# A block of four mixers and a gated FFN on one core: one difference of the fast down projection made later, five of its chunks moved ahead of the last pair's values, and another order in the input norm

## Chip, cores and metric

One Trainium2 chip, one of its cores. The metric is the time of one execution on the device in microseconds (us), as the median of the runs of a kernel; all numbers of the trace come from one profiled execution. The engines have short names in the profile: PE is TensorE (matmuls), PEld its weight loads, DVE is VectorE, ACT is ScalarE, POOL is GpSimd, SP is SyncE, which here only issues DMAs. A "q" behind a name is the engine's sequencer.

## What is computed

One layer over 1024 tokens of width 1024, in float32. Four mixers, the gates, two norms and the FFN; what matters here is the input norm and the FFN.

```python
h = rms_norm(x, norm_mix_g)
proj = h @ w_in                    # all branches and the gates
...                                # four mixers, gated and merged
x = x + merged @ w_out
h = rms_norm(x, norm_ffn_g)

def conv_ffn(h, w_up, conv_w, conv_b, w_down):
    up = causal_dwconv(h @ w_up, conv_w) + conv_b
    val, gate = jnp.split(up, 2, axis=-1)
    return (jax.nn.silu(gate) * val) @ w_down

x = x + conv_ffn(h, ffn_w_up, ffn_conv_w, ffn_conv_b, ffn_w_down)   # D_FF = 2816
return rms_norm(x, norm_final_g)
```

## The kernel before

**Number format.** Every float32 operand of a large matmul is split into a rounded high part and the rest (`split`, L153: a cast, then a subtraction of 128x512), and a product is three matmuls: high by high, low by high, high by low. Tiles named `...hi` and `...lo`, `th` and `tl` are such parts. Channels lie on the partitions, tokens along the free axis.

**Order of the work.** The program is traced in Python order, and a scheduler then lays out each engine's queue at compile time: an instruction that stands earlier in the program has the higher priority, and a later one may be put ahead of it where the scheduler expects the earlier one to have to wait. On the chip every engine runs its own queue in order. A tile's buffer is reused when its last reader is done; pools that are opened after others have closed take their memory.

**Input norm** (`norm_in`, L349). x comes in two halves of 512 tokens. For each half x times the gain is split unscaled, the products of block B_DN and of the first two gate blocks are made from it, and only then the row scale is known (`rms_scale`, a sum of squares by PE and a chain of twelve small VectorE instructions); `spread_scale` brings it to the rows by eight small matmuls, and the products are scaled behind (`scaled`). `rescale` (L406) multiplies x by gain and scale and splits it again for all later products: the cast on ScalarE, the low part on VectorE for k = 0, 3, 6 and on GpSimd for the five others. `ab_out` (L422) scales and transposes a small product (tile `abf`).

**Up projection** (`ffn_up`, L1598). 22 pairs of blocks (i = 0 to 21), each by a fast 2x2 scheme with seven products instead of eight (`seven`, L1557), in PSUM tiles `qa` and `qb` with two buffers each, so that one pair computes while the one before is read out. `pair_weights` makes and splits the weights of a pair, mostly on GpSimd. `hidden` (L1622) turns a pair into values: the convolution and the gating on VectorE and ScalarE, a store to `gd[i]`, and on GpSimd the differences which the down projection wants: `td[0]` for i under 11 (N_HALF), `td[1]` and `td[2]` from 11 on (L1636 to L1642), and in each even i two combinations of down weights, `sd[0]` and `sd[1]`.

**Down projection** (`ffn_down`, L1677). The same 2x2 scheme over halves of D_FF, of the output channels and of the tokens: seven products of eleven chunks, a chunk being twelve matmuls. `parts` loads one or two sources into raw buffers, subtracts if there are two, and splits. `raw` (L1689) rotates the raw buffers: eight places r, f, f, s, r, f, s, f, of which r has two buffers (shared with the up projection), f and s three each; after the first product every second load goes to one of eight buffers `raws` of the pool `down`, which takes the memory of the up projection's pool. Weights' parts rotate over seven buffers (`w_slot`); the other side's over six of the pool `down` (`own="t"`), but in the first product over the seven as well. `G[0]` and `G[1]` are the two sets of PSUM tiles. The last product holds its last six chunks back and runs them in two token quarters, with the final norm between.

Of the kernel before, what the change touches and what calls it, by code (L numbers as in the profile page):

```python
# [11 lines left out]
F32 = mybir.dt.float32  # L12
# [17 lines left out]
N_HALF = N_FF // 2  # L30
LEAD = 24
N_HELD = 6
S5_G = 16
# [65 lines left out]
class Builder:  # L99
# [249 lines left out]
    def norm_in(self):  # L349

        nc = self.nc
        with ExitStack() as st:
# [24 lines left out]
            for f, s in enumerate(halves):  # L377
                for k in range(NK):
                    self.scale_split(xs[f][:, k, :], g[:, k:k + 1], self.h_hi[:, k, s], self.h_lo[:, k, s], nc.vector)
                dn.append(self.products(self.early[B_DN], s, self.ps("pd")))  # L380
                ab = self.ab_products(w_ab, s)
                ssq = self.t(xp, [P, 512], F32, "ssq", 2)
                for k in range(NK):
                    x = xs[f][:, k, :]
                    sq = ssq if k == 0 else self.t(xp, [P, 512], F32, "rms_sq", 4)
                    nc.scalar.activation(sq, x, AF.Square)
                    if k:
                        nc.vector.tensor_tensor(ssq, ssq, sq, op=ALU.add)
                r = self.rms_scale(xp, ssq, self.ones, 1.0 / 1024, f"rs{f}")
                self.spread_scale(r, f)  # L390
                if f:
                    self.rescale(xs[0], g, 0)
                o = [self.products(self.early[B_GATE], s, self.gate_ps()), self.products(self.load_in(B_GATE + 1), s, self.ps())]
                if f:
                    self.rescale(xs[1], g, 1)
                for i in range(2):
                    self.gate_out(i, s, self.scaled(o[i], s))
                self.ab_out(xp, ab, s, f)
            self.started = {B_GATE + 2: [self.products(self.load_in(B_GATE + 2), halves[0], self.gate_ps())]}
            self.started[B_DN + 2] = [self.products(self.load_in(B_DN + 2), halves[0], self.ps())]  # L400
            self.started[B_DN] = [self.scaled(o, s) for o, s in zip(dn, halves)]
# [4 lines left out]
    def rescale(self, x, g, f):  # L406

        nc = self.nc
        s = slice(512 * f, 512 * f + 512)
        for k in range(NK):  # L410
            nc.vector.scalar_tensor_tensor(x[:, k, :], x[:, k, :], g[:, k:k + 1], self.rt[:, s], op0=ALU.mult, op1=ALU.mult)
            self.split(self.h_hi[:, k, s], self.h_lo[:, k, s], x[:, k, :], nc.scalar, nc.vector if k % 3 == 0 else nc.gpsimd)

# [971 lines left out]
    def build(self):  # L1385
# [42 lines left out]
        self.gd = [self.t(self.dp, [P, L], F32, f"gd{k}") for k in range(N_FF)]  # L1428
        self.sd, self.td = ([[self.t(self.dp, [P, 512], F32, f"{x}{i}{k}") for k in range(N_HALF)] for i in range(n)] for x, n in (("sd", 2), ("td", 3)))
        with ExitStack() as sx, ExitStack() as st:  # L1430
# [12 lines left out]
            with ExitStack() as s1:  # L1443
                self.ffn_up(ctx, sx, st, s1, xs, ssq, late)
        self.ffn_down(ctx)

# [150 lines left out]

    def ffn_up(self, ctx, sx, st, s1, xs, ssq, late):  # L1598

# [22 lines left out]
        def hidden(i, q):  # L1622
# [15 lines left out]
            g.dma_start(self.td[i // N_HALF][k], t)  # L1638
            if i >= N_HALF:
                t4 = self.t(fp, [P, 512], F32, "tu", 5)  # L1640
                g.tensor_tensor(t4, val[:, 0:512], t, op=ALU.subtract)
                g.dma_start(self.td[2][k], t4)  # L1642
            if i % 2 == 0:
# [27 lines left out]
        for i in range(1, N_FF):  # L1671
            j = job(i)
            for _ in j[2]:
                pass
            hidden(*j[:2])

    def ffn_down(self, ctx):  # L1677

        nc = self.nc
        v, g = nc.vector, nc.gpsimd
        pool = self.pool(ctx, "down", side="left")
        halves = slice(0, 512), slice(512, 1024)
# [3 lines left out]
        def raw(src):  # L1689
            i = next(n_raw)  # L1690
            r = flat(self.raw_slot("rffsrfsf"[i % 8])) if i < 2 * N_HALF or i % 2 else self.t(pool, [P, 512], F32, "raws", 8)
            nc.sync.dma_start(r, src)
            return r
# [17 lines left out]
        def A(a, b):  # L1711
            return lambda k: self.a["w_dn"][N_HALF * b + k][:, halves[a]]
# [5 lines left out]
        T = lambda i: lambda k: self.td[i][k]  # L1718
        G = [[x[:, h] for x in self.banks() for h in halves] for _ in range(2)]
        def add(f, c, ps, s=slice(0, 512)):  # L1720
# [73 lines left out]
        two, xs = [[], []], [[], []]  # L1794
        product(G[0], [A(0, 0)], [B(0, 0)], True, own=None)
        residual(0, 0)
        product(G[1], [A(0, 1)], [B(1, 0)], True, between={5: adds(0, 0, G[0]), 7: lambda: residual(1, 0)})
        product(G[0], [S(1)], [T(1)], False, between={3: adds(0, 0, G[1]), 4: lambda: residual(1, 1)})
# [23 lines left out]

        kept = product(G[0], [A(1, 1)], [T(2)], False, N_HELD, between={1: last})
        early = totals(squares(0, range(4), every), 1)[0]
# [97 lines left out]
```

## Time and profile before

| | us |
|---|---|
| median of 3 runs | 1717.28 (1715.68 to 1718.93) |
| the profiled execution, its own time | 1719.06 |
| its span, from the first to the last instruction | 1717.3 |
| up projection, about | 1046 to 1478 |
| down projection and final norm, about | 1478 to 1717 |

The page of the profile gives shares of the span by engine; a table by stretches gives each engine's busy time in a window of time, and how many instructions it ran; the chain of waits goes back from the last instruction through whatever released each step; the timeline lists one engine's instructions with start and duration. PE's matmuls are pipelined: a 128x512 matmul is shown 0.39 us long, but the next starts 0.227 us later at the full clock, and twelve take 2.72 us.

### The profile page before, as it was taken

The numbers are of one execution on the slowest core, as the hardware profiler recorded it, in microseconds if no ns is written. First come the engines' busy times: TensorE is split into PE (matmuls) and PEld (weight loads), VectorE is DVE, ScalarE is ACT, GpSimd is POOL, SyncE is SP. The second block draws the span as 40 slices with busy tenths as digits, with TensorE's granted clock in tenths as the row PEclk, the third lists the DMA queues.
The fourth block names the chain that finished last, engine by engine and source line by source line (L and its number), as shares of the span: only waits on it lengthen the run. The fifth ranks groups of instructions, "written<-read, shape, count | busy, mean of one in ns | idle before, by whom it ended". The sixth has DMA issues, their size and how long they took to land.

```text
span 1717.3 us, 22540 instructions
## 1 busy us (share of the span) xinstructions
PE 1641.2 (96%) x7762; PEld 1321.3 (77%) x7762; DVE 1256.2 (73%) x2265; ACT 678.4 (40%) x1219; POOL 645.1 (38%) x571
## 2 busy tenths in 40 slices
PE   7899999989999999999999999999998989999996
PEld 5686776766787877778888787788887777778886
DVE  8895966777623749795578667888878888855785
ACT  4342332212332336564213445454443434444353
POOL 2412033344310222211001425988999898300002
PEclk9899999999999999999999999999999999999998
DMA  4113222213432673414755442433344344687763
GB/s 156 66 64 90 60 83 70 90 64 78 149 130 98 137 141 90 102 50 150 275 201 172 141 141 66 143 123 128 135 142 148 135 147 148 219 306 242 246 213 104
DMA packets 137955, 233.64 MB, mean 136 GB/s; under 512 B 42785, under 2 KB 51745, under 8 KB 137329
## 3 DMA queue, kind: packets, MB, share of 16 engines
q1 hardware_dynamic: 105072, 151.26, 28.4%
q10 hardware_dynamic: 17968, 54.37, 8.7%
q0 software_dynamic: 14800, 26.58, 6.0%
q8 instruction: 61, 1.00, 0.2%
q14 instruction: 54, 0.43, 0.1%
HBM read 164.69 MB, written 66.85 MB: 135 GB/s over the span
## 4 chain that ended last, share of the span: by engine, by line
PE 68%; DVE 10%; DMA 3%; issue 3%; POOL 2%; ACT 2%; SPq 0%; DVEq 0%; POOLq 0%; ACTq 0%
PE qb L92 16%; PE pd L92 15%; PE qa L92 14%; PE pg L92 13%; PE ps L92 6%; DVE glo L155 2%; PE ps L96 1%; PE p L92 1%; DVE cg L1628 1%; DMA fr<-sd 1%; DMA fr<-gd 1%; ACT p L1029 0%; DMA raws<-in_w_dn_dram 0%; POOL x L1772 0%; DVE wlo L155 0%
## 5 line engine op out<-in xcount | busy, mean ns | idle before, releaser
L155 POOL TENSOR_TENSOR glo<-raw,ghi 128x512 fp32r<-128x512 f32 x72 | 98.3, 1368 | 361.7 <-ACT ghi L148 348.5
L92 PE MATMUL pg<-hhi,ghi 128*128 128x512 f32 x496 | 207.2, 418 | 0.0
L92 PE MATMUL pg<-hlo,ghi 128*128 128x512 f32 x496 | 198.9, 401 | 0.0
L92 PE MATMUL pg<-hhi,glo 128*128 128x512 f32 x496 | 198.8, 401 | 0.0
L92 PE MATMUL pd<-hhi,whi 128*128 128x512 f32 x312 | 128.2, 412 | 2.0 <-ACT silt L511 1.9
L92 PE MATMUL pd<-hhi,wlo 128*128 128x512 f32 x312 | 122.4, 392 | 2.0 <-DVE wlo L155 2.0
L92 PE MATMUL pd<-hlo,whi 128*128 128x512 f32 x312 | 122.2, 392 | 0.0
L148 ACT CAST ghi<-raw 128x512 fp32r<-128x512 f32 x97 | 59.9, 618 | 152.6 <-DVE cv L1629 75.8
L92 PE MATMUL qa<-xh,ghi 128*128 128x512 f32 x264 | 105.4, 399 | 14.9 <-DVE qa L1587 14.9
L92 PEld LDWEIGHTS pg<-hhi,ghi 128*128 128x128 f32 x496 | 95.1, 192 | 23.1 <-issue 6.7
L92 PEld LDWEIGHTS pg<-hlo,ghi 128*128 128x128 f32 x496 | 95.2, 192 | 19.3
L92 PEld LDWEIGHTS pg<-hhi,glo 128*128 128x128 f32 x496 | 95.5, 192 | 15.8 <-issue 0.3
L92 PE MATMUL qa<-xh,glo 128*128 128x512 f32 x264 | 104.4, 395 | 0.0
L92 PE MATMUL qa<-xl,ghi 128*128 128x512 f32 x264 | 104.3, 395 | 0.0
L92 PE MATMUL qb<-xh,whi 128*128 128x512 f32 x264 | 103.1, 391 | 1.2 <-ACT whi L148 0.8
L92 PE MATMUL qb<-xh,wlo 128*128 128x512 f32 x264 | 102.7, 389 | 0.0
L92 PE MATMUL qb<-xl,whi 128*128 128x512 f32 x264 | 102.7, 389 | 0.0
L148 ACT CAST whi<-raw 128x512 fp32r<-128x512 f32 x90 | 55.9, 621 | 89.2 <-PE pd L92 53.4
L155 DVE TENSOR_TENSOR wlo<-raw,whi 128x512 fp32r<-128x512 f32 x61 | 46.7, 767 | 39.1 <-ACT whi L148 38.9
L92 PEld LDWEIGHTS pd<-hhi,whi 128*128 128x128 f32 x312 | 58.8, 189 | 20.0 <-ACT silt L511 3.8
L1340 ACT ACTIVATE gate<-pg 128x512 f32<-128x512 f32 x62 | 37.1, 599 | 92.5 <-PE pg L92 91.8
L92 PEld LDWEIGHTS qa<-xh,ghi 128*128 128x128 f32 x264 | 50.6, 192 | 27.9 <-DVE qa L1587 17.4
(716 smaller groups left out, 4554.7 us busy)
## 6 DMA issues: line engine op xcount, KB each, us to landing
raw<-in_w_in_dram SPq DMA_DIRECT2D x104, 256.0 KB
gates<-gate ACTq DMA_DIRECT2D x32, 512.0 KB
gld<-gates ACTq DMA_DIRECT2D x32, 512.0 KB
fr<-in_w_up_dram SPq DMA_DIRECT2D x44, 256.0 KB
raw<-in_w_up_dram SPq DMA_DIRECT2D x44, 256.0 KB
gd<-cv ACTq DMA_DIRECT2D x22, 512.0 KB
raws<-in_w_dn_dram SPq DMA_DIRECT2D x44, 256.0 KB
tu<-in_w_dn_dram SPq DMA_DIRECT2D x33, 256.0 KB
```

The source lines that it names most:

```text
L92: return self.nc.tensor.matmul(out, w, x, **kw)
L96: return self.nc.tensor.transpose(out, x, ident)
L148: eng.copy(out, in_)
L155: (e_lo or self.nc.vector).tensor_tensor(lo, src, hi.bitcast(F32), op=ALU.subtract)
L1340: self.nc.scalar.activation(self.gt[i][:, s], ps, AF.Tanh, scale=0.5)
L1628: v.scalar_tensor_tensor(gate, t, 1.0, gate, op0=ALU.add, op1=ALU.mult)
```

## The change

It has three parts. In the input norm, the products of the first gate block come ahead of `spread_scale`, `ab_out` of the second half comes behind the products of the third gate block, and all low parts of `rescale` go to VectorE. In the FFN, `td[2]` is no longer made in `hidden`; the last product loads `gd` and `td[1]` and subtracts them itself. And `ffn_down` becomes a generator that `ffn_up` steps: five chunks of its first product (EARLY) come ahead of `hidden` of the last pair, the other six behind it; the second product then takes all its buffers from the places that the first one uses, and the pool `down` is opened after the first.

```diff
+EARLY = 5
...
                 r = self.rms_scale(xp, ssq, self.ones, 1.0 / 1024, f"rs{f}")
+                o = [self.products(self.early[B_GATE], s, self.gate_ps())]
                 self.spread_scale(r, f)
                 if f:
                     self.rescale(xs[0], g, 0)
-                o = [self.products(self.early[B_GATE], s, self.gate_ps()), self.products(self.load_in(B_GATE + 1), s, self.ps())]
+                o.append(self.products(self.load_in(B_GATE + 1), s, self.ps()))
...
-                self.ab_out(xp, ab, s, f)
+                if f == 0:
+                    self.ab_out(xp, ab, s, f)
             self.started = {B_GATE + 2: [self.products(self.load_in(B_GATE + 2), halves[0], self.gate_ps())]}
+            self.ab_out(xp, ab, s, 1)
...
-            self.split(self.h_hi[:, k, s], self.h_lo[:, k, s], x[:, k, :], nc.scalar, nc.vector if k % 3 == 0 else nc.gpsimd)
+            self.split(self.h_hi[:, k, s], self.h_lo[:, k, s], x[:, k, :], nc.scalar, nc.vector)
...
-                self.ffn_up(ctx, sx, st, s1, xs, ssq, late)
-        self.ffn_down(ctx)
+                down = self.ffn_down(ctx)
+                self.ffn_up(ctx, sx, st, s1, xs, ssq, late, down)
+        for _ in down:
+            pass
...
             g.dma_start(self.td[i // N_HALF][k], t)
-            if i >= N_HALF:
-                t4 = self.t(fp, [P, 512], F32, "tu", 5)
-                g.tensor_tensor(t4, val[:, 0:512], t, op=ALU.subtract)
-                g.dma_start(self.td[2][k], t4)
...
             for _ in j[2]:
                 pass
+            if i == N_FF - 1:
+                next(down)
             hidden(*j[:2])
+        next(down)
...
-            r = flat(self.raw_slot("rffsrfsf"[i % 8])) if i < 2 * N_HALF or i % 2 else self.t(pool, [P, 512], F32, "raws", 8)
+            r = flat(self.raw_slot("rffsrfsf"[i % 8])) if i < 4 * N_HALF or i % 2 else self.t(pool, [P, 512], F32, "raws", 8)
...
-        product(G[0], [A(0, 0)], [B(0, 0)], True, own=None)
+        for k in range(N_HALF):
+            if k == EARLY:
+                yield
+            run(G[0], parts([A(0, 0)(k)]), parts([B(0, 0)(k)]), k == 0, k == N_HALF - 1)
+        yield
+        G.append([x[:, h] for x in self.banks() for h in halves])
+        pool = self.pool(ctx, "down", side="left")
         residual(0, 0)
-        product(G[1], [A(0, 1)], [B(1, 0)], True, between={5: adds(0, 0, G[0]), 7: lambda: residual(1, 0)})
+        product(G[1], [A(0, 1)], [B(1, 0)], True, own=None, between={5: adds(0, 0, G[0]), 7: lambda: residual(1, 0)})
...
-        kept = product(G[0], [A(1, 1)], [T(2)], False, N_HELD, between={1: last})
+        kept = product(G[0], [A(1, 1)], [B(1, 0), T(1)], False, N_HELD, between={1: last})
```

## Rows read from the trace of the kernel before

**Rows 1.** The page: busy us, share and instructions of PE; the chain by engine.
```profile
PE 1641.2 (96%) x7762; PEld 1321.3 (77%) x7762; DVE 1256.2 (73%) x2265; ACT 678.4 (40%) x1219; POOL 645.1 (38%) x571
PE 68%; DVE 10%; DMA 3%; issue 3%; POOL 2%; ACT 2%; SPq 0%; DVEq 0%; POOLq 0%; ACTq 0%
```
**Rows 2.** Stretches of the up projection: window and length, each engine's busy us (instructions), PEclk, DMA, GB/s.
```profile
1215.00:1253.00 38.00, 38.00 (x169) 31.48 (x168) 30.39 (x27) 18.08 (x27) 34.62 (x27) 1.00 0.39 132
1291.00:1334.00 43.00, 38.30 (x160) 31.17 (x159) 34.07 (x25) 16.33 (x25) 39.76 (x33) 0.92 0.41 141
```
**Rows 3.** The chain of waits in order of time: start, duration, what.
```profile
1290.64 2.72 PE qa L92 x12
...
1309.68 2.73 PE qa L92 x12
...
1315.09 7.32 DVE cg L1628
...
1440.44 2.73 PE qa L92 x12
...
1461.61 2.72 PE qa L92 x12
```
**Rows 4.** VectorE's groups by line, 1101 to 1291 us: count, busy us, mean ns, idle before.
```profile
L1628 DVE SCALAR_TENSOR_TENSOR cg<-ct,cg 128x1024 f32<-128x1024 f32 x10 | 20.2, 2024 | 1.4 <-ACT ct L1627 1.4
```
**Rows 5.** Timeline of POOL: start, duration, instruction, idle before and what ended it.
```profile
1304.99 1.31 POOL L1641 TENSOR_TENSOR tu<-cv,tu 128x512 f32<-128x512 f32 x1
1306.59 0.56 POOL L1642 DMA_DIRECT2D td<-tu  x1 [0.30 <-POOL tu L1641]
...
1315.05 1.30 POOL L1550 TENSOR_TENSOR fs<-raw,fr 128x512 f32<-128x512 f32 x1
...
1320.04 1.27 POOL L155 TENSOR_TENSOR wlo<-fs,whi 128x512 fp32r<-128x512 f32 x1
```
**Rows 6.** Stretches of 10 us at the seam, columns as in the second group.
```profile
1500.00:1510.00 10.00, 6.20 (x26) 4.50 (x26) 3.95 (x7) 3.63 (x8) 0.67 (x1) 1.00 0.84 285
1510.00:1520.00 10.00, 9.76 (x35) 7.62 (x36) 8.53 (x15) 6.44 (x12) 0.00 (x0) 0.83 0.93 311
1520.00:1530.00 10.00, 10.00 (x45) 8.27 (x45) 6.90 (x14) 4.57 (x8) 1.41 (x2) 1.00 0.99 349
```
**Rows 7.** PE's waits from 1478 to 1515 us: us in total, times, longest.
```profile
PE qa L92 <- ACT whi L148: 3.5, 1, 3.5
```
**Rows 8.** The chain of waits at the seam.
```profile
1500.44 7.08 DMA fr<-gd
```
**Rows 9.** The page's costliest groups: a cast of the split.
```profile
L148 ACT CAST whi<-raw 128x512 fp32r<-128x512 f32 x90 | 55.9, 621 | 89.2 <-PE pd L92 53.4
```
**Rows 10.** PE's waits from 0 to 130 us.
```profile
PE ps L92 <- DVE rs1y L236: 3.4, 1, 3.4
PE ps L96 <- DVE abf L426: 3.2, 1, 3.2
```
**Rows 11.** Stretches of the input norm, columns as in the second group.
```profile
53.30:60.10 6.80, 5.92 (x18) 5.08 (x19) 3.34 (x8) 2.34 (x4) 1.39 (x1) 0.50 0.12 40
70.40:77.20 6.80, 5.84 (x17) 4.63 (x18) 5.46 (x33) 2.77 (x6) 0.76 (x1) 0.50 0.87 293
...
80.00:120.00 40.00, 39.83 (x189) 32.40 (x188) 38.50 (x158) 18.13 (x34) 2.88 (x2) 1.00 0.18 58
```
**Rows 12.** The instructions on the tile `raws`: duration ns min/median/max, first and last start.
```profile
L1708 DVE TENSOR_TENSOR raws<-raws,fr x17: 683/685/693, 1584.8 to 1649.2; 128x512 f32<-128x512 f32 x17
```
**Rows 13.** VectorE's groups by line, 40 to 72 us.
```profile
L411 DVE SCALAR_TENSOR_TENSOR x<-x,cols,rt 128x512 f32<-128x512 f32 x14 | 15.3, 1131 | 2.8 <-ACT rt L404 2.8
L155 DVE TENSOR_TENSOR hlo<-x,hhi 128x512 fp32r<-128x512 f32 x6 | 6.8, 1130 | 0.5 <-ACT hhi L148 0.5
```
**Rows 14.** Timeline of VectorE ahead of 40 us.
```profile
37.14 0.74 DVE L411 SCALAR_TENSOR_TENSOR x<-x,cols,rt 128x512 f32<-128x512 f32 x1
```
**Rows 15.** The stretch of the last product's splits, columns as in the second group.
```profile
1650.00:1682.00 32.00, 31.82 (x150) 26.44 (x149) 30.09 (x49) 23.73 (x45) 0.00 (x0) 1.00 0.44 149
```

More of the change, by code (lines that the diff above doesn't have):

```diff
@@ L1428, in build @@
         self.gd = [self.t(self.dp, [P, L], F32, f"gd{k}") for k in range(N_FF)]
-        self.sd, self.td = ([[self.t(self.dp, [P, 512], F32, f"{x}{i}{k}") for k in range(N_HALF)] for i in range(n)] for x, n in (("sd", 2), ("td", 3)))
+        self.sd, self.td = ([[self.t(self.dp, [P, 512], F32, f"{x}{i}{k}") for k in range(N_HALF)] for i in range(2)] for x in ("sd", "td"))
         with ExitStack() as sx, ExitStack() as st:
@@ L1595, in banks, with ffn_up @@
         return [self.t(self.pp, [P, L], F32, x, 2) for x in ("qa", "qb")]
-    def ffn_up(self, ctx, sx, st, s1, xs, ssq, late):
+    def ffn_up(self, ctx, sx, st, s1, xs, ssq, late, down):
         nc = self.nc
@@ L1683, in ffn_down @@
         v, g = nc.vector, nc.gpsimd
-        pool = self.pool(ctx, "down", side="left")
         halves = slice(0, 512), slice(512, 1024)
@@ L1718, in ffn_down @@
         T = lambda i: lambda k: self.td[i][k]
-        G = [[x[:, h] for x in self.banks() for h in halves] for _ in range(2)]
+        G = [[x[:, h] for x in self.banks() for h in halves]]
         def add(f, c, ps, s=slice(0, 512)):
```

## The prediction, made before the changed kernel was built or run

> **What bounds the kernel now.** I read the page first [rows 1]: TensorE (PE) is busy 96% of the span, and it makes up 68% of the span in the chain that ended last. So a change is worth what it takes out of PE's idle time, and the next view is the table by stretches of the up projection [rows 2]. Two pairs of blocks take 38 us there while PE has no idle (169 matmuls in 38 us); from 1291 us on the same work takes 43 us, with fewer matmuls in it. The chain in order of time [rows 3] tells what PE waits for: it runs through PE alone from pair to pair, 19.04 us each (1290.64 to 1309.68), and then, once in two pairs, through one instruction of VectorE (DVE), the first of them 7.32 us long. The ten of its line (L1628) from 1101 to 1291 us take 2.02 us in the mean [rows 4]. The timeline of GpSimd (POOL) beside it [rows 5] says why: from 1315.05 on five of POOL's additions stand end to end to 1321.3, and VectorE's instruction ends only after them. POOL had no pause left: what it does since pair 11 and did not do before is the early-made difference T(2), L1640 to L1642.
>
> The other two places where PE loses time are the input norm (before 80 us) and the seam between up and down projection (near 1500 us); the last product is where the change puts work.
>
> **Part 1, the difference that leaves the pairs.** Removed in each of pairs 11 to 21: one POOL addition (1.31 us), the 0.30 us before its store and the issue of 0.56 us [rows 5], so 2.17 us of POOL a pair, 4.3 us in two. In pairs 0 to 10 POOL is busy 34.6 us of 38 [rows 2], so 4.3 more makes 38.9, over 38; without T(2) pairs 11 to 21 put on POOL what pairs 0 to 10 put on it, where PE lost nothing. The removed stores also leave the DMA queues (41% busy there [rows 2], so no gain is booked). What the stalls cost, clock included: six pairs from 1309.68 to 1440.44 take 130.76 us, against 6 x 19.04 = 114.24; that is 16.5; the pair from 1440.44 to 1461.61 takes 21.17, 2.1 more [rows 3]. **Sum: -18.6 us**, all of it on PE's path. Ends: -18.6, and -15 if one stall of the smaller size and a half stay.
>
> One rule speaks against this term. The Trainium skill (SBUF — State Buffer, "SBUF: two separate sides") says that VectorE and GpSimd share a port pair as a lock which is held for one instruction: the loser waits for that instruction. By it VectorE would wait 1.3 us here, not 7.3, a full POOL queue would not matter, and part 1 would be worth little; that is rival D below. The trace disagrees so far: 7.32 us spans five POOL instructions.
>
> **Part 2, the last pair's values behind five chunks.** The chunks of the first product of the down projection now stand ahead of the last `hidden` on every queue (SP's loads, ScalarE's casts, VectorE's splits); behind them wait the last pair's convolution on VectorE and ScalarE, its store of `gd` and of its `td`, wanted by the last chunks of the second and third products, over 40 us later, the release of its PSUM banks, wanted at the second product, and POOL's loads of the residual, which need the pool's memory and are wanted in its fifth chunk. So the wait itself costs nothing while the six later chunks cover it (6 x 2.72 = 16.3 us, a chunk being twelve matmuls [rows 3]). What could be gained: at 45 matmuls in a full 10 us, the two stretches from 1500 to 1520 with 26 and 35 miss 29, that is 6.4 us [rows 6]. But PE's one named wait of weight there is 3.5 us [rows 7], for the last chunk, and the chain puts it down to a load of `gd` that took 7.08 us to land [rows 8], while DMA was 84 to 99% busy [rows 6]: a queue of transfers, not the last pair's values. The change does take five early loads into the `raws` buffers away from there, but it also leaves the second product with eight load buffers instead of sixteen and with seven split buffers for both sides. Four of eight places in the list `rffsrfsf` are f, with three buffers: one f load a chunk. With a landing of 7.08, a cast of 0.62 [rows 9] and a split of 0.69 an f buffer comes round in 8.4 us, against 8.16 for three chunks on PE: 0.1 us a chunk, 1 us in all, 2 with some queueing. Ends -6.4 and +2; I take **-2.5**, nearer to the middle, since half of the crowd of transfers remains.
>
> **Part 3, the input norm.** PE waits 3.4 us for the scale of the second half (rs1y) and 3.2 us for `abf` [rows 10], and after each it ran 6.8 us at a granted clock of 0.50 [rows 11], the 1.2 GHz level: of 5.92 and 5.84 us busy, half is loss. Exposed: 3.4 + 3.2 + 3.0 + 2.9 = 12.5 us. The change puts 24 matmuls ahead of the first wait (20 stood there already, four are new) and 17 more ahead of the second (17 x 0.227 = 3.9 us, enough to cover 3.2). It moves ten low-part subtractions (five in each half) from POOL to VectorE: 10 x 0.685 [rows 12] = 6.9 us more on VectorE. But beside POOL's subtractions VectorE's own are drawn out: from 40 to 72 us fourteen multiplications of L411 take 1.131 us in the mean and six subtractions 1.130 [rows 13], against 0.74 for one of L411 ahead of that [rows 14] and 0.685: 14 x 0.39 + 6 x 0.445 = 8.1 us, and with no low part left on POOL that goes. Net: VectorE -1.2 us there. Its second rescaling waits for the scale's rows from PE, and these would come up to 3.4 us sooner, as the small instructions of the scale are drawn out likewise; four fifths of it, some 2.8 us, look within reach. A last 1 us is the idle time that VectorE spends now between the two. What is late next is VectorE: in 80 to 120 us it is busy 38.5 of 40 [rows 11], so PE cannot run ahead of it for long, and I book VectorE's lead, 1.2 + 2.8 + 1 = **-5 us**, not the 12.5. Ends: -12.5 and +6.9 (all ten subtractions exposed, nothing recovered). A gain here moves everything behind it, whose order on the queues is fixed.
>
> **Part 4, the difference in the last product.** Eleven loads of 256 KB and eleven VectorE subtractions are added where `T(2)` was read. From 1650 to 1682 us VectorE is busy 30.09 of 32 [rows 15]; a subtraction of this form takes 0.685 [rows 12]: 11 x 0.685 = 7.5 us, of which 1.9 fit into idle time. DMA is 44% busy in that stretch [rows 15] and takes the loads. The splits of the last held chunk would end some 5 us later than now, and the chain of small instructions for the first final scale stands behind or among them; PE's half-width matmuls reach these chunks with about 2 us in hand. So 3 us of stall and one stretch of half clock: **+4 us**. Ends 0 (the subtractions fit in front of the splits, which wait for PE anyway) and +10 (all 7.5 exposed, and a half-clock stretch as in part 3).
>
> **Sum.** -18.6 - 2.5 - 5 + 4 = -22.1 us. The profiled execution took 1719.06 us, of which the span is 1717.3; it gives 1697.0. It stands 1.8 us above the median of 1717.28; from that median it is **1695 us**.
>
> **Rivals.**
> - B, what is put behind takes half back: nothing in the norm, +2 at the seam, +8 in the last product. For it: VectorE is nearly full in both places it is loaded. Against: the parts that are late there also lose contention. -18.6 + 2 + 8 = -8.6: 1709 us.
> - C, PE is free in the norm and at the seam: -18.6 - 6.4 - 10 + 2 = -33: 1684 us. For it: no named wait remains there. Against: VectorE at 38.5 of 40.
> - D, the long VectorE instructions are not POOL's streak: if each conflict is one instruction long, the stalls stay when T(2) goes, -22.1 + 18.6 = -3.5: 1714 us. Against: the stalls begin with pair 11 and have a period of two pairs, as POOL's load has.
> - E, slower: the second product starves on its three f buffers. The other terms make -19.6, so it decides from 1.8 us a chunk more over eleven chunks on, that is (2.72 + 1.8) x 3 = 13.6 us for three chunks, a landing of 12 us; at 15 us three chunks take 16.6, 2.8 us more for each, and the time is 1717 - 19.6 + 31 = 1729 us. For it: DMA was 99% busy in the 10 us after the seam [rows 6]. Against: the landing read there is 7.08 us.
> - That part 2 does nothing is in the terms (its zero): product one follows the last pair without a gap already.
>
> **How the numbers follow.** Forecast 0.57 (1689 to 1701), B 0.22 (1702 to 1713), C 0.13 (1680 to 1688), D 0.04, E 0.04. The range 1685 to 1709 leaves out half of C, a third of B, D and E. About 0.2%, 3.4 us, is what a measurement of this kernel can tell from no change: faster 0.93 (all but E and half of D, with a little of B), same 0.03, slower 0.04.
>
> **What would show it.** Part 1: in the chain no VectorE row over 4 us in the up projection, all pairs 19.04 us apart. Part 2: full windows of 45 matmuls from the last pair to the end of the second product; a new PE wait for f loads there is B or E. Part 3: no PE wait on rs1y or abf over 1 us, no half clock from 53 to 77 us, no subtraction over 0.8 us; PE waits between 60 and 120 us would tell that VectorE is late. Part 4: VectorE busy without a break in the last 60 us, PE waiting for the splits of held chunks or for the scale. Wrong altogether if the pairs still pause once in two.

## The result, and the profile after

The changed kernel takes 1699.01 us, the median of four runs (1694.99 to 1702.13), against 1717.78 of the kernel before (four runs beside them): ratio 0.9891, 95% interval 0.9868 to 0.9914, so 18.8 us less. The forecast was 1695, its range 1685 to 1709. The profiled execution took 1694.99 us, with a span of 1693.2; it is the fastest of the four, so the two traces lie 24 us apart where the medians lie 18.8 apart. The sums below go by the medians for that reason, and the traces say where the time went.

Both kernels run the same 7762 matmuls, so a stretch can be measured from one matmul of a given number to another, in the timeline of PE. "Input norm" is number 150 to 600, "mixers" 600 to 1800, "merge" 4050 to 4500 (the gated outputs are merged ahead of the output projection), "pairs" 5850 to 6750 (pair 11 to the first chunks of the down projection), "seam" 6750 to 7200, "last" 7200 to the start of the last one. 900 matmuls without a pause at the full clock take 204.1 us. (The stretches that are left out differ by 0.5 us at most between these two.)

```
us              norm   mixers  merge   pairs   seam    last
before         114.59  260.84  104.05  222.65  109.14  114.80
after          105.23  259.35  107.59  204.71  104.15  121.97
```

The page: busy us, share and instructions of PE, and the chain by engine (before: [rows 1]).

```profile
PE 1628.4 (96%) x7762; PEld 1313.0 (78%) x7762; DVE 1229.8 (73%) x2286; ACT 677.7 (40%) x1219; POOL 602.9 (36%) x539
...
PE 72%; DVE 13%; DMA 7%; issue 3%; POOL 2%; ACT 2%; SPq 0%; DVEq 0%; ACTq 0%; POOLq 0%
```

The pairs, by stretches (window and length, busy us and instructions of PE, PEld, DVE, ACT, POOL, granted clock, DMA share, GB/s) and in the chain of waits; before: [rows 2, 3].

```profile
1291.00:1329.00 38.00, 38.00 (x169) 31.50 (x168) 29.61 (x28) 18.32 (x27) 31.35 (x24) 1.00 0.44 141
...
1372.96 5.44 PE qb L93 x24
...
1392.00 5.44 PE qb L93 x24
```

Two pairs take 38 us for 169 matmuls again, one pair following the other after 19.04 us, and no VectorE row is left in the chain there. (For 20 us, from 1331 to 1351, the chain runs through POOL and two transfers; PE's longest wait from 1060 to 1460 us is 0.7 us.)

The input norm: two groups of VectorE from 40 to 72 us, PE's wait, and stretches (before: [rows 10, 11, 13]).

```profile
L156 DVE TENSOR_TENSOR hlo<-x,hhi 128x512 fp32r<-128x512 f32 x16 | 11.1, 724 | 0.4 <-ACT hhi L149 0.4
L415 DVE SCALAR_TENSOR_TENSOR x<-x,cols,rt 128x512 f32<-128x512 f32 x14 | 9.8, 743 | 1.3 <-ACT rt L408 1.3
```
```profile
PE ps L93 <- DVE rs1y L237: 1.2, 1, 1.2
```
```profile
53.30:60.10 6.80, 5.96 (x30) 5.13 (x31) 5.40 (x12) 4.19 (x7) 0.08 (x1) 1.00 0.25 81
70.40:77.20 6.80, 6.80 (x32) 5.61 (x31) 6.49 (x47) 2.33 (x5) 0.00 (x0) 1.00 0.43 138
...
80.00:120.00 40.00, 39.87 (x191) 32.08 (x190) 39.27 (x138) 17.26 (x31) 6.16 (x3) 1.00 0.18 57
```

The clock is full where it was 0.50, VectorE's instructions have about the length they have without POOL beside them ([rows 12, 14]: 0.685 and 0.74 us), and from 80 to 120 us VectorE is busier than before (39.27 of 40) while PE is busy 39.87. The wait for the scale of the second half is down from 3.4 to 1.2 us, and the one for `abf` is gone.

The seam: stretches of 10 us (before: [rows 6]).

```profile
1470.00:1480.00 10.00, 10.00 (x45) 8.26 (x45) 4.58 (x7) 3.62 (x7) 1.45 (x2) 1.00 0.91 289
1480.00:1490.00 10.00, 9.41 (x39) 6.88 (x38) 5.55 (x10) 4.37 (x8) 0.00 (x0) 1.00 0.93 324
1490.00:1500.00 10.00, 10.00 (x45) 8.27 (x45) 5.76 (x12) 3.99 (x8) 0.00 (x0) 1.00 0.69 227
```

The weakest ten us have 39 matmuls where they had 26, with transfers as dense as before (0.91 and 0.93 busy).

The end: PE's waits from 1590 to 1690 us, stretches, and the chain of waits.

```profile
PE qa L93 <- DVE x L1727: 5.6, 2, 5.0
```
```profile
1620.00:1630.00 10.00, 9.51 (x42) 7.39 (x41) 5.03 (x9) 3.65 (x7) 0.00 (x0) 1.00 0.84 273
1630.00:1640.00 10.00, 5.00 (x22) 3.91 (x21) 8.81 (x15) 3.94 (x7) 0.00 (x0) 0.86 0.73 233
1640.00:1650.00 10.00, 10.00 (x37) 8.04 (x37) 10.00 (x18) 5.65 (x11) 0.00 (x0) 0.80 0.54 175
```
```profile
1614.28 3.35 DMA fr<-sd
...
1620.28 4.06 DMA fr<-td
...
1625.78 4.39 DMA fr<-td
...
1631.55 2.68 DMA fr<-gd
```

Before, PE's longest wait from 1600 to 1695 us was 0.6 us. Now it stands 5.0 us at 1634, and the granted clock of the two windows falls to 0.86 and 0.80; it waits for additions (L1727) that read out PSUM, and these stand on VectorE's queue behind subtractions and splits that wait for loads to land. From 1620 to 1630 VectorE is busy only 5.03 of 10: it is not full, it is waiting.

### The profile page after: what moved, and what is told of

Same layout as the page of the kernel before. It is cut to its first block, busy times and chain, and to the rows that moved or that the text cites. A ratio compares the mean times of both kernels' runs of the same rounds, so it can differ in the third digit from the quotient of the medians.

```text
span 1693.2 us, 22524 instructions
## 1 busy us (share of the span) xinstructions
PE 1628.4 (96%) x7762; PEld 1313.0 (78%) x7762; DVE 1229.8 (73%) x2286; ACT 677.7 (40%) x1219; POOL 602.9 (36%) x539
## 4 chain that ended last, share of the span: by engine, by line
PE 72%; DVE 13%; DMA 7%; issue 3%; POOL 2%; ACT 2%; SPq 0%; DVEq 0%; ACTq 0%; POOLq 0%
PE pd L93 19%; PE qb L93 16%; PE pg L93 13%; PE qa L93 13%; PE ps L93 8%; PE ps L97 2%; PE p L93 1%; DMA raws<-in_w_dn_dram 1%; DMA fr<-td 1%; DMA raw<-in_w_in_dram 1%; DMA fr<-sd 1%; DVE osb L680 1%; DVE glo L156 1%; DMA fr<-gd 1%; DVE row L681 1%
## 5 line engine op out<-in xcount | busy, mean ns | idle before, releaser
L93 PEld LDWEIGHTS pg<-hlo,ghi 128*128 128x128 f32 x496 | 93.5, 188 | 18.8
L93 PEld LDWEIGHTS pd<-hhi,wlo 128*128 128x128 f32 x312 | 58.7, 188 | 12.6 <-DVE wlo L156 2.5
```

The lines of the kernel that those rows point to most:

```text
L93: return self.nc.tensor.matmul(out, w, x, **kw)
```

## The experiments

All medians are beside runs of the kernel before on the same chip (1716.96 to 1717.20). The stretches are those of the profiled execution of each.

```
                                  median  ratio to before [95%]       norm   mixers  merge   pairs   seam    last
part 1, T(2) not made             1697.86 0.9896 [0.9875, 0.9916]   114.45  259.70  104.14  204.72  106.29  113.72
parts 1 and 4                     1707.53 0.9945 [0.9928, 0.9963]   115.02  260.00  107.60  204.18  105.08  123.63
part 2                            1718.32 1.0012 [1.0000, 1.0024]   115.17  260.86  106.79  222.57  108.78  113.92
part 3                            1712.73 0.9977 [0.9965, 0.9989]   105.40  264.07  103.88  209.43  110.92  113.58
part 3, another execution         1714.92 one run                   105.44  264.16  107.56  223.13  109.42  112.77
part 3, low parts alone           1710.88 0.9964 [0.9951, 0.9977]   105.65  260.26  107.69  221.17  109.22  114.01
parts 1, 3 and 4                  1700.08 0.9897 [0.9880, 0.9914]   105.19  263.79  108.46  204.30  104.26  121.23
after, last product without load  1691.63 0.9853 [0.9836, 0.9870]   105.82  259.89  103.76  204.19  106.53  117.32
after, T(2) early on VectorE      1719.95 1.0019 [1.0005, 1.0034]   105.39  260.41  103.83  234.72  106.35  113.14
after, the same one pair late     1700.35 0.9910 [0.9891, 0.9929]   105.79  263.79  103.90  212.68  107.18  114.23
after, memsets on POOL            1713.45 0.9977 [0.9963, 0.9991]   105.23  262.81  103.61  221.19  103.90  123.24
after, POOL's addition, no store  1706.80 0.9945 [0.9925, 0.9965]   105.55  264.66  103.91  211.57  105.81  120.06
```

### Part 1 alone

```diff
-            if i >= N_HALF:
-                t4 = self.t(fp, [P, 512], F32, "tu", 5)
-                g.tensor_tensor(t4, val[:, 0:512], t, op=ALU.subtract)
-                g.dma_start(self.td[2][k], t4)
...
-        kept = product(G[0], [A(1, 1)], [T(2)], False, N_HELD, between={1: last})
+        kept = product(G[0], [A(1, 1)], [T(1)], False, N_HELD, between={1: last})
```

> The kernel before without the early-made difference T(2): no POOL addition and no store for it from pair 11 on; the last product reads T(1) in its place, so one subtraction of the result is left out and the number of loads in the last product stays as before. Theory (POOL without a pause draws out VectorE's instruction): pairs 11 to 21 run 19.04 us apart, the stalls of 16.5 + 2.1 us go, nothing else moves: -17 to -19 us, 1699 to 1701 us. Rival (the long VectorE instructions come from something else, and what took them away in the whole change was its other parts): 1714 to 1718 us, with VectorE rows of 7 us still once in two pairs.

This kernel leaves the difference T(2) out of the layer. Measured: 0.9896, that is 17.9 us less. The pairs lose their 18 us of stalls, and the seam becomes 2.9 us shorter as well, with part 2 not in. The rival fell.

### Parts 1 and 4

As the kernel above, with the changed kernel's last product: `[B(1, 0), T(1)]`.

> As the run without T(2), but the last product loads gd and T(1) and subtracts them itself, with the buffers of the kernel before (a pool of eight raws and six t parts open from the start). Against that run: theory L (what is added in the last product costs 7.5 us whatever the rest, since its loads share buffers and DMA queues with those of the product ahead): +7 to +8 us, 1706 to 1709 us, with PE waiting some 5 us for a split behind a landing early in the last product. Rival B (it costs because the order and the buffers of part 2 leave the loads late): 0 to +3 us. Rival V (VectorE being full, as in my prediction): +3 to +5 us, and the pause lies at the held chunks, in the last 50 us.

Measured: 9.7 us over the run above by the medians, 8.4 by the ratios (0.9945 - 0.9896 = 0.0049 of 1717), and "last" is 9.9 us longer. PE stands 5.6 us, once, for an addition of L1718 (L1727 of the changed kernel); its waits from 1590 to 1700 us:

```profile
PE qa L92 <- DVE x L1718: 6.4, 3, 5.6
```

Theory L holds by the place, early in the last product, and lies a little under the measured size; what PE waits for is an addition behind a split, not the split. Part 2's buffers are not needed for it, so rival B fell. Stretches at the same times (the second kernel starts "last" 2.8 us later), first without T(2), then with the subtraction in the last product:

```profile
1632.00:1642.00 10.00, 10.00 (x46) 8.28 (x45) 9.44 (x17) 5.18 (x10) 0.00 (x0) 1.00 0.88 309
1642.00:1652.00 10.00, 10.00 (x46) 8.29 (x45) 9.69 (x16) 9.52 (x19) 0.00 (x0) 1.00 0.15 43
```
```profile
1632.00:1642.00 10.00, 9.30 (x41) 7.36 (x40) 5.70 (x10) 3.64 (x7) 0.00 (x0) 1.00 0.80 244
1642.00:1652.00 10.00, 5.67 (x26) 4.35 (x24) 7.57 (x13) 3.94 (x7) 0.00 (x0) 0.99 0.74 237
```

Without the added loads the transfers are done at 1642 (0.15 from there); with them transfers go on at 237 GB/s for ten more us. VectorE is busy 5.70 of 10 from 1632 and 7.57 from 1642, where it was 9.44 and 9.69.

### The loads or VectorE

In the changed kernel, the subtraction of the last product becomes an addition of its first operand to itself, and T(1) is neither loaded nor used:

```diff
-            v.tensor_tensor(x, x, raw(srcs[1]), op=ALU.subtract)
+            v.tensor_tensor(x, x, raw(srcs[1]) if srcs[1] is not None else x, op=ALU.add if srcs[1] is None else ALU.subtract)
...
-        kept = product(G[0], [A(1, 1)], [B(1, 0), T(1)], False, N_HELD, between={1: last})
+        kept = product(G[0], [A(1, 1)], [B(1, 0), lambda k: None], False, N_HELD, between={1: last})
```

> The changed kernel, but in the last product the operand loaded from gd is added to itself instead of T(1) being loaded and subtracted: the eleven VectorE instructions stay, the eleven loads of 256 KB go (so the last product's operand is another one). Theory (the loads are the cost: the queue of transfers is 80 to 90% busy ahead of the last product): -6 to -8 us against the changed kernel, 1691 to 1693 us. Rival (VectorE's eleven instructions are the cost, as in my prediction): 0 to -3 us, 1696 to 1699 us.

Measured: 1691.63, and 0.9853 against 0.9891: 6.5 us less than the changed kernel with all eleven VectorE instructions still in. So the loads are most of the cost: 6.5 of part 4's 8.4 us. The 1.9 us that are left would be the subtractions', but that is less than the runs resolve, and in the traces "last" is only 4.7 us shorter without the loads. PE's wait of 5.0 us is down to 0.9, and at the same place the transfers keep the DMA engines 0.56 busy:

```profile
PE qa L93 <- DVE x L1727: 0.9, 1, 0.9
```
```profile
1628.00:1638.00 10.00, 9.07 (x40) 7.24 (x39) 8.22 (x14) 2.19 (x4) 0.00 (x0) 1.00 0.56 176
```

### Part 2 alone, and everything but part 2

The first kernel has only the hunks of `ffn_down` and `ffn_up` that belong to the early chunks and their buffers, the second has all the others.

> Only the order at the seam and its buffers: five chunks ahead of the last pair's values, the second product on the buffers of the first, the pool opened later. T(2), its use and the input norm as in the kernel before. Theory (the gain of 5 us read between matmuls 6750 and the second product in the comparison of the traces is this part's own): -4 to -6 us, 1712 to 1714 us. Rival (it is there only because the stalls of the pairs are gone, POOL and the DMA queues being freer): -2 to +1 us, 1716 to 1719 us.

> The whole change but part 2: the last pair's values stand ahead of the down projection and the pool is open from the start, as before. In the run of part 2 alone nothing was gained, while the comparison of the traces showed 5 us at the seam. Theory (most of these 5 us come with the pairs' stalls going: the runs without T(2) gained 3 to 4 us there without part 2): the changed kernel's time plus 1 to 2 us, 1700 to 1702 us. Rival (part 2 is worth its 5 us as soon as the stalls are gone): 1703 to 1705 us. Rival (part 2 costs, by its fewer buffers): 1696 to 1698 us.

Measured: alone 1.0012, no gain; its seam is 0.4 us shorter than before's, and PE still waits there for a cast behind a load of `gd`, 4.7 us where it was 3.5 [rows 7, 8]:

```profile
PE qa L93 <- ACT whi L149: 4.7, 1, 4.7
```
```profile
1510.04 7.72 DMA fr<-gd
```

So the theory of the first expectation fell and its rival's time came. Everything but part 2 takes 0.9897 against 0.9891 for the whole: 1 us, within both intervals. Its seam is 104.26 us, the whole change's 104.15. So the 5 us that the seam lost between the two traces did not come with part 2: the five kernels without a stall in the pairs have a seam of 104.2 to 106.5 us, three of them without part 2 and two with it. The time of the second expectation's theory came and its rivals' did not; the intervals alone, some 3 us each way, would not decide between them, the seams do.

The theory's reason is half right. It is not the stalls' going that shortens the seam: the memsets further down make the pairs stall again (221.19 us) with the shortest seam of all, 103.90, and T(2) made on VectorE gives 234.72 and 106.35. All five kernels in which POOL makes and stores T(2) have 108.8 to 110.9 us, the nine others 103.9 to 107.2. What counts there is that POOL no longer does this work; with its addition back but not its store the seam is 105.81, so the addition alone does not bring the long seam back.

### Part 3 alone, and its low parts alone

```diff
-            self.split(self.h_hi[:, k, s], self.h_lo[:, k, s], x[:, k, :], nc.scalar, nc.vector if k % 3 == 0 else nc.gpsimd)
+            self.split(self.h_hi[:, k, s], self.h_lo[:, k, s], x[:, k, :], nc.scalar, nc.vector)
```

is the whole edit of the run of the low parts; the run of part 3 has the two moves in `norm_in` as well.

> Only the input norm's three edits. Theory (the norm's own stalls go; 9.8 us by 160 us of the span, 2 more by 480, and 3.5 are given back where the gates are merged ahead of the output projection): -8 to -9 us, 1709 to 1710 us. Rival 1 (the 3.5 us at the merge are not a consequence of the norm but of that run): -11 to -12 us, 1706 us. Rival 2 (my term, VectorE's lead of 5 us): 1712 us. The window 53 to 77 us should be without half clock in either.

> Only the low parts of the input norm's rescaling on VectorE, with the order of before. Theory (the order hides the two waits, and the low parts on VectorE only make its instructions shorter): -1 to -4 us at matmul 450 of PE, against -8.3 with the order, the half clock after the waits stays. Rival (VectorE drawn out beside POOL's subtractions made both waits): -7 to -9 us there with the order as before, and no half clock from 53 to 77 us.

> A second look at the input norm's three edits alone, whose eleven executions lay between 1701 and 1717 us while its profile was the fastest of them. Theory (the order of every queue from 290 us on is that of the kernel before, so the pairs' stalls are the same work meeting at another phase, and differ from execution to execution): at 120 us of the span -8 to -9 us against before as in the first look, by 1050 us -4 to -9, and stalls in the pairs of 11 to 22 us in all, unlike the 5 us in the first look. Rival (an earlier input norm takes stalls out of the pairs): stalls of 3 to 6 us again.

Measured: the norm becomes 9 us shorter in all three, 105.40, 105.44 and 105.65, and the theory of the low parts' run fell: they alone bring all of it, and no half clock is left.

```profile
53.30:60.10 6.80, 5.56 (x29) 4.42 (x29) 5.37 (x11) 4.01 (x7) 1.16 (x1) 1.00 0.31 97
70.40:77.20 6.80, 6.80 (x32) 5.61 (x31) 6.03 (x37) 1.96 (x5) 0.00 (x0) 1.00 0.61 187
```

Beside the low parts the two moves change nothing: in the traces of part 3 and of the low parts alone each engine runs the same instructions in the same order, so the scheduler lays out the order of the changed program text by itself as soon as the low parts are on VectorE. (The moves without the low parts were not run.) The two kernels are therefore one program measured twice, 0.9977 and 0.9964: 4 to 6 us less, not 9. The theory of the first expectation fell; the time of its rival 2 came, but not for rival 2's reason, since the norm itself did give 9 us. Two things stand between. In the mixers, six of the ten profiled executions with the new norm take 262.8 to 264.7 us, the other four 259.4 to 260.4, and the four with the old norm 259.7 to 260.9. All ten with the new norm have a pause of PE of 2.4 us at one matmul near 270 us, which the old norm has not; in the six, the granted clock falls to 0.50 within 2 us of its end and stays there for 3.4 to 6.8 us, in the four it does not. So this loss comes with the new norm, in some executions. And the merge takes either about 104 or 106.8 to 108.5 us, in kernels of both kinds: what looked like 3.5 us given back there in the changed kernel is no consequence of the change.

The pairs in part 3 are the other surprise. From 290 us on, the order of every queue is that of the kernel before; yet its first execution lost 5 us in the pairs, the other one 19. From the chain of waits of the first (two rows of VectorE over 3 us from 1300 to 1420 us), then of the other:

```profile
1310.15 4.82 DVE cg L1631
...
1389.87 3.51 DVE cg L1631
```
```profile
1312.27 7.29 DVE cg L1631
...
1356.23 4.58 DVE glo L155
...
1398.23 7.30 DVE cg L1631
```

The same work meets at another phase. So the third expectation's theory holds for the stalls (19 us, in its range of 11 to 22); at 1050 us this execution was 2.9 us ahead of before, less than the 4 to 9 that it gave, as its mixers and its merge took 3.3 and 3.5 us more. A single profile does not size such a stall.

### What in POOL's work draws the stalls

Two kernels put work back on POOL in pairs 11 to 21 of the changed kernel: four memsets, which read nothing, and T(2)'s addition without its store.

```diff
+            if i >= N_HALF:
+                t4 = self.t(fp, [P, 512], F32, "tu", 5)
+                for _ in range(4):
+                    g.memset(t4, 0.0)
```
```diff
+            if i >= N_HALF:
+                t4 = self.t(fp, [P, 512], F32, "tu", 5)
+                g.tensor_tensor(t4, val[:, 0:512], t, op=ALU.subtract)
```

> The changed kernel with four POOL memsets of 128x512 in each of pairs 11 to 21 where the addition for T(2) stood (a row of the kernel before has such a memset at 0.53 us, so 2.1 us a pair, as much as T(2) took with its store; they read nothing). Theory F (what counts is that POOL has no pause left): the stalls return, +10 to +19 us against the changed kernel. Theory A (what counts is additions that read two operands end to end: while a memset runs VectorE gets its turn): 0 to +3 us, and no VectorE row over 4 us in the up projection.

> The changed kernel with POOL's addition for T(2) back in pairs 11 to 21, but not its store: 1.3 us a pair instead of 2.17. With four memsets a pair in its place the time came back (+14 us), yet no VectorE row was over 2.3 us: PE waited for POOL's low parts of weights. Theory S (additions end to end draw out VectorE's reads): VectorE rows over 4 us in the up projection again and 3 to 12 us lost. Theory F (what decides is how late POOL is with the weights, which 1.3 us a pair don't make): 0 to +2 us against the changed kernel, no VectorE row over 4 us.

Measured: both cost time, +14.8 us with the memsets (0.9977 against 0.9891) and +9.3 with the addition (0.9945), but in two ways. With memsets no VectorE row of this line is over 2.4 us from 1270 to 1460 us (shortest, median and longest in ns), and PE waits for POOL itself, for low parts of weights (waits from 1291 to 1380 us):

```profile
L1634 DVE SCALAR_TENSOR_TENSOR cg<-ct,cg x10: 1210/1226/2318, 1272.0 to 1460.0; 128x1024 f32<-128x1024 f32 x10
```
```profile
PE qb L93 <- POOL glo L156: 4.4, 3, 1.6
```

So time came back as theory F said, though not through VectorE, and the rows are as theory A said. The kernel before took the other way: from 1291 to 1478 us PE waited for VectorE alone.

```profile
PE qa L92 <- DVE qa L1587: 13.1, 4, 5.1
```

With the one addition there are VectorE rows of 4.2 to 4.6 us again, once in two pairs, and POOL is busy 37.4 of the 40 us that two pairs now take, beside pauses of 0.30 us ahead of stores:

```profile
1308.46 4.21 DVE glo L156
...
1348.10 4.60 DVE glo L156
...
1388.12 4.57 DVE glo L156
```
```profile
1336.00:1376.00 40.00, 38.35 (x170) 31.43 (x169) 32.88 (x26) 18.04 (x26) 37.37 (x29) 1.00 0.41 140
```

Theory S holds: beside additions that stand end to end VectorE's instructions are drawn out, and 1.3 us a pair more of them are enough for it. The pairs lose 6.9 us by it and the seam 1.7. That is less than half of the 17.9 us that the pairs lost in the kernel before; the store and the 0.30 us ahead of it, or another phase, make the rest, which no run tells apart.

### T(2) early, but on VectorE

Two tries to keep part 1's gain without part 4's price. The first puts T(2) on VectorE at once (`v.tensor_tensor`, stored from SP, with the last product of the kernel before); the second one pair later:

```diff
...
+            if i > N_HALF:
+                b, x, kk = self.lag
+                one = self.t(fp, [P, 1], F32, "one", 2)
+                v.tensor_scalar(one, gate[:, 0:1], 0.0, 1.0, op0=ALU.mult, op1=ALU.add)
+                v.scalar_tensor_tensor(x, b[:, 0:512], one, x, op0=ALU.mult, op1=ALU.subtract)
             v.tensor_tensor(val, val, gate, op=ALU.mult)
             nc.scalar.dma_start(self.gd[i], val)
+            if i > N_HALF:
+                nc.scalar.dma_start(self.td[2][kk], x)
...
+            self.lag = val, t, k
...
```

> The changed kernel, but T(2) is made early again, on VectorE instead of POOL, and stored from SP; the last product reads it as the kernel before did. Theory (part 4 costs 7.5 us by its loads, and VectorE, busy 28 to 30 us of 38 for two pairs, has room for 1.4 us more): -6 to -8 us against the changed kernel, 1691 to 1693 us, no pause of PE in the last product before the final norm, pairs 19.04 us apart. Rival 1 (another instruction of two reads on VectorE meets POOL's additions, and PE waits for the pair's values again): 1700 to 1710 us. Rival 2 (a store on SP's queue, which waits for VectorE, holds up the loads of weights behind it): 1697 to 1705 us, with PE waiting for weights in the pairs.

> The changed kernel with T(2) made early on VectorE, but one pair late: behind the product of the next pair's values, when POOL's difference td[1] of this pair has long been there (pinned by a factor of one taken from the next pair's gate), stored from ScalarE behind the store of gd; the last pair's on POOL as in the kernel before. In the run with T(2) on VectorE at once, VectorE waited 2.4 us in each pair for POOL's td[1], with everything PE wanted queued behind it. Theory (that wait was the whole loss, and the loads of the last product cost 7): no wait of VectorE for POOL in pairs 12 to 20, pairs 19.04 us apart, no pause of PE ahead of the last product's held chunks, -6 to -8 us against the changed kernel, 1690 to 1693 us. Rival 1 (any further VectorE instruction with two operands from SBUF is drawn out by POOL's additions and holds up the pairs): 1700 to 1712 us. Rival 2 (the values are kept a pair longer in three buffers, so ScalarE's next convolution waits): pairs of 20 us and more, 1705 to 1715 us.

Measured: the first takes 1.0019, as long as the kernel before and longer than any case of its expectation. VectorE waits for POOL's difference in every pair (four of them from 1291 to 1380 us), and what PE wants stands behind; none of those cases had named that wait:

```profile
DVE tu L1647 <- POOL tu L1643: 9.6, 4, 2.4
```

The second takes 0.9910, the time of the changed kernel (0.9891 to within the intervals). It does win "last" back, 114.23 against 121.97, but the pairs pay 8.0 and the seam 3.0 us: the new instruction has no one to wait for, but it stands in front of the readout that PE waits for (L1593), and at 1.77 us in the chain (0.74 at its shortest) it is drawn out beside POOL's additions.

```profile
1336.91 1.77 DVE tu L1639
1338.68 0.62 DVE qa L1593
...
1357.01 1.77 DVE tu L1639
1358.78 0.62 DVE qa L1593
```

Rival 1 of the second expectation has place and time. No kernel here that computes the whole layer beats the changed one.

## Why the prediction was right, and where it was not

**The sum.** -22.1 was forecast, the runs say -18.8. By the ratios: part 1 -17.9, part 4 +8.4, part 3 -8.2 (parts 1, 3 and 4 against 1 and 4) beside those two and -4 to -6 alone, part 2 -1. The mechanism that carries the time, part 1, was right in place and size; the miss of 3.3 us is mostly part 4's, partly paid by part 3. That the sum came closer than its terms is luck: part 4 cost 4.4 us more than forecast, and part 3 gave 3.2 more. The intervals of two ratios leave 4 to 5 us on each of these differences, so the split rests on the traces as well.

**Part 1, -18.6: right.** -17.9 in the runs, 17.9 in the pairs between the traces (222.65 to 204.71); the chain has no VectorE row over 4 us, as forecast. Rival D fell with it. What the step did not see: the seam becomes 3 to 4 us shorter by it, and the order of before can lose 5 us or 19 in the pairs from one execution to the next, so that a term read from one profile carries several us either way.

On the rule weighed there the runs say more than the trace before did. A VectorE instruction of 0.7 us took 4.60 beside one further POOL addition a pair, and none was over 2.32 beside memsets. The Trainium skill (SBUF — State Buffer, "SBUF: two separate sides") gives the shared ports to whichever starts first for its whole instruction, and the other blocks. Read as the prediction read it, that the loser waits for one instruction, these rows disagree for additions that stand end to end, and the measurement decides.

**Part 2, -2.5: too much.** Alone it brings nothing, beside the others 1 us at most. The step that failed is where half of the 6.4 us was booked to the five loads that moved: the load of `gd` behind which PE's cast waits still takes 7.72 us to land (7.08 before). Where the seam did get shorter, it was part 1's doing. The cost that the range of this term allowed for (+2) and rival E did not come: the changed kernel has no pause of over 0.6 us from the seam to 1634 us. (Rival E's arithmetic was a little off: with the cast and the split, a landing of 15 us makes 16.3 us for three chunks, not 16.6, and so 1728 us.)

**Part 3, -5: right in the sum, for a wrong reason.** The stretch itself gave 9.4, nearer to the end of -12.5 than to the term; the runs of this part alone gave 4 to 6, since the mixers give part of it back in six executions of ten. Two steps failed. "so PE cannot run ahead of it for long" did not hold: VectorE is busy 39.27 of 40 from 80 to 120 us and PE keeps its lead. And the 24 and 17 matmuls that were to cover the waits were no edit of their own: the scheduler placed them as soon as the low parts had moved. The lengths of instructions came out nearly as read, 743 and 724 ns against 740 and 685. Of the signs named for this part the half clock went; two waits for scales, of 1.2 and 1.1 us, stayed just over the 1 us set for them.

**Part 4, +4: mis-sized, and the wrong resource.** It costs 8.4 us, 6.5 of them for the loads. The step that failed is that DMA "is 44% busy in that stretch [rows 15] and takes the loads". That window, 1650 to 1682 us [rows 15], is where the product is computed; its loads are issued while the product ahead of it still loads. The kernel before, in two windows there:

```profile
1643.00:1653.00 10.00, 9.66 (x42) 7.35 (x41) 7.87 (x14) 4.05 (x7) 0.00 (x0) 1.00 0.75 252
1653.00:1663.00 10.00, 10.00 (x46) 8.27 (x45) 9.99 (x17) 5.19 (x9) 0.00 (x0) 1.00 0.96 339
```

Eleven loads of 256 KB are 2.88 MB; as an estimate, that is 8.5 us of transfers at the 339 GB/s of the second window and 12 at 240. The pause came before the held chunks, not at them, and VectorE waited rather than being full. As an estimate by the Trainium skill's table (DMA: Bandwidth & Descriptors, "Bandwidth"), at its 341 GB/s for transfers of 1 MB, they would take 8.5 us too. The trace agrees with that rate, though its loads are of 256 KB: windows that are over 0.9 busy, here and in [rows 6], moved 289 to 349 GB/s.

Bytes are not all of it. Around the pause of the changed kernel the DMA engines are 0.84, 0.73 and 0.54 busy, so they were not full. Each of the four loads into `fr` in the chain is issued within 0.1 us of the end of a VectorE instruction that read one of the three `fr` buffers, and SP, which issues them, has a wait from 1590 to 1660 us, for buffers that come free only with the added subtraction, which neither the kernel before nor the run without the loads has:

```profile
SPq L1697 <- DVE fr L1713: 4.1, 2, 3.5
```

So landing, subtraction and the next load follow one another, as rival E feared for the second product. The run without the loads frees their buffers too; whether more buffers alone would take the cost away was not run.

Rival B's time did not come, though its +8 in the last product did: what it denied to the norm came. C had the norm's stretch nearly right, but put 6.4 us of gain on the seam and only +2 on part 4.

## What to carry to other kernels

Price an added load in the stretch in which it is issued, not in the one in which its data is used, by its bytes and by the buffer it has to wait for, and look at what a queue holds up behind its landing: here 2.88 MB cost 6.5 us because a readout stood behind them. Work that is moved to an engine with idle time still stands in front of something: ask which instruction follows it on that queue and who waits for that one. And when an edit has several lines, build the smallest of them alone before explaining the rest: the scheduler may already do what the others ask for.

## What the runs showed of the hardware

The granted clock does not follow from a pause alone. In the kernel of part 3 and in the one of its low parts, the same program, PE pauses 2.4 us at the same matmul near 268 us (waiting for VectorE's `state`); the stretch behind it then ran at 0.77 in one execution (6.8 us of it at 0.50, the lower of the two levels, 1.2 GHz) and at 1.00 in the other, with the longer mixers in the first (264.07 against 260.26):

```profile
270.00:285.00 15.00, 14.36 (x56) 10.76 (x57) 9.40 (x30) 2.74 (x7) 1.41 (x3) 0.77 0.18 57
```
```profile
270.00:285.00 15.00, 12.75 (x63) 9.44 (x64) 10.32 (x32) 2.75 (x7) 2.23 (x5) 1.00 0.21 66
```

56 matmuls in the first take 14.36 us of busy time, 63 in the second 12.75. A spread of some us between executions of one kernel comes out of such places: of the ten executions with this pause, the six with the half clock behind it have the longer mixers, and the four without it the shorter. Why the clock falls in one and not in the other stays open.
